# A sample's recurrence in two wide units, shift states stored in rows, and a layer norm in the dense PSUM banks

## The chip, the cores and the metric

The kernel runs on one core of a Trainium2 chip. The metric is the time on the device of one execution, in microseconds (us), less being better. A core has five engines with an instruction queue each: TensorE (PE in the profile, with its weight loads as PEld), VectorE (DVE), ScalarE (ACT), GpSimd (POOL) and SyncE (SP), which here issues nearly all the DMAs. Each engine takes its instructions in order, and waits between engines go by semaphores. Matmul results land in PSUM, eight banks of 128 partitions by 512 fp32 numbers, from where DVE and ACT read them.

## The reference

One step of a two-layer encoder, on a new prompt of 1024 tokens and on 64 further tokens of a running stream, the sample, whose states are inputs. The model is 1024 wide. Layer 0 mixes tokens by two recurrences side by side, RWKV-7 with eight heads of 64 and a gated linear attention (GLA) with four heads, both fed by one input projection; their outputs, joined, go through one output projection. Layer 1 mixes them by attention over a band of chunks. Behind each mixer stand a residual with a layer norm, a SwiGLU feed-forward part (FFN), and again a residual with a layer norm. Besides the two outputs, all end states are returned. The change touches the recurrence, two of its returned states and one layer norm.

```python
def wkv7_scan(r, decay, k, v, kk, a, S0):
    def step(S, inp):
        r_t, w_t, k_t, v_t, kk_t, a_t = inp
        sa = jnp.einsum('bhvk,bhk->bhv', S, kk_t)
        S = (S * w_t[:, :, None, :] - sa[..., None] * (kk_t * a_t)[:, :, None, :]
             + v_t[..., None] * k_t[:, :, None, :])
        return S, jnp.einsum('bhvk,bhk->bhv', S, r_t)
...
def rwkv7_time_mix(pa, shift0, wkv0, mu, ...):
    prev = jnp.concatenate([shift0[:, None, :].astype(pa.dtype), pa[:, :-1]], axis=1)
    xs = pa + (prev - pa) * mu
    ...
    wkv, o = wkv7_scan(r, decay, k, v, kk, a, wkv0)
    ...
    return y, wkv.astype(wkv0.dtype), pa[:, -1]
```

`pa` is the part of the input projection that feeds RWKV, 1792 columns. Its last row, `pa[:, -1]`, is the **shift state**, returned once for the prompt and once for the sample.

## The kernel before

*Halves.* The tokens are worked in two halves. Half 0 holds the first 384 prompt tokens and the 64 of the sample (448 columns), half 1 the other 640 prompt tokens. `run` (L1340) writes the program down in this order: input projection of half 0, the scan of half 0 beside the rest of its projection, input projection of half 1, output projection of half 0 with layer norm ln1, FFN of half 0 with the scan of half 1 beside it, and so on. The Tile scheduler then sets the order of the instructions on each engine by its own model of time, so that instructions of parts that are independent mix.

*Dense matmuls.* Each is split into fp32r high and low parts and done as three products: `gemm_ws` (L124 to L126, weights stationary) and `gemm_ts` (L135 to L138, tokens stationary), with weights loaded by SP (L98) and split by ACT (L101), DVE (L106) and POOL (L108). They write in a pool of three PSUM banks, which `self.bank()` hands out (tile name gps). The output projection adds into the accumulators acc (L825, L827 and L829), which are loaded from the input by SP (acc<-in_x).

*The recurrence.* `rwkv` (L656) splits the eight heads into four pairs p and the tokens into chunks of 64. A unit is one pair and n chunks. Units go through a pipeline of five steps, one step of each of five units in a round: `rw1` (L412: loads rkv, xg and rsb through SP, gate matmuls in the bank pa, elementwise work), `rw1b` (products in pb and pt), rw2 (an inverse of triangular 16 by 16 blocks: the write of lab to l_d in DRAM, its diagonal blocks read back as lt, and 15 rounds of a DVE product and sum, L549 and L551; more in pz), `rw3` (L599: the state S goes through the unit's chunks in the bank ps) and `rw4` (L645: output y, written to yg_d). For the prompt n is 2, one pair and two chunks, so all tiles are 128 wide. The sample has one chunk: four units of n = 1, one for each pair, 64 wide, which stand ahead of the prompt's units of half 0. With three pairs of chunks in half 0 and five in half 1, there are 4 + 12 + 20 = 36 units. A step of the GLA (`gla`, tiles named g...) is drawn beside each round.

*Scan banks.* The scan has PSUM banks of its own, by tags: pa, pb and pt share one, pz has one, ps and py share two, and everything else, the GLA's and "tps", shares one. `self.tpsum` says where the transposes of a layer norm (L902) and a few others land: from L1350 on in the bank "tps". ACT (L113) and DVE (L114) then split them into xh and xl for the next matmuls.

*Shift states.* `shift_evac` copies the last column of each of the 14 projection tiles into a column of a tile of 128 by 14: shS in half 0 (the sample's), shP in half 1 (L290). At the end of half 1's projection both are stored as 1792 numbers, transposed by the DMA's access pattern (L1377 and L1378). The scheduler moves the store of shS ahead to 92 us.

*What follows half 1's projection.* SP has the write rkv_d<-xs (L303), the loads of the scan (rkv, L427; xg; rsb), loads and stores of the value cache (cv, L1125, and vd, L1128, with ACT's and DVE's split of cv as cvh), the read of yg_d as yraw, whose split xh (L215) and xl (L216) is the output projection's input, and the loads of acc.

## Time and profile before

| what | before |
|---|---|
| runs (us) | 3109.51, 3102.37, 3113.97; median 3109.51 |
| the profiled execution: time, span (us) | 3102.95, 3101.2 |
| mean granted TensorE clock | 0.977 |
| DMA packets, bytes | 298492, 399.29 MB (mean 129 GB/s) |
| share of the chain that ended last, by engine | PE 77%, DVE 8%, DMA 7%, POOL 2%, ACT 2%, issue 2%, SP's queue 1% |

The span runs from the first to the last instruction. A busy time is the sum over an engine's instructions; PE and PEld overlap. The granted clock is the share of full speed that the throttle allowed PE. A group's line gives the line of the code, the engine, the operation and its tiles. "<-" in a list of waits names what ended an engine's idle time. The chain of waits is followed back from the last instruction: at each step to what released it, or to the instruction before it on its engine.

### The profile page before, as it was taken

The page shows a single profiled execution, that of the slowest core. Times are in us where ns is not written, and L with a number is a line of the kernel's source. Part 1 is how long each engine was busy: PE and PEld are TensorE (multiplying, and loading weights), DVE is VectorE, ACT ScalarE, POOL GpSimd, SP SyncE. Part 2 cuts the span into 40 slices and gives each one's busy share as a digit, 9 for nine tenths or more (in the row PEclk, how much of TensorE's full clock was granted, in tenths as well). Part 3 has the DMA queues.
Part 4 walks back from the last instruction along what each step waited for, and adds up shares of the span by engine and source line. Part 5 has one row for each costly group of instructions (what it writes and reads, how often), then busy time and mean ns, then how long its engine had stood idle before and what let it go on. Part 6 is the DMA issues. An engine that isn't in the chain of part 4 may idle for free.

```text
span 3101.2 us, 50069 instructions
## 1 busy us (share of the span) xinstructions
PE 3007.5 (97%) x17468; PEld 2676.5 (86%) x17468; DVE 2016.0 (65%) x4941; ACT 1270.8 (41%) x2761; POOL 1366.7 (44%) x1489
## 2 busy tenths in 40 slices
PE   8999999899999999999999999999999999899998
PEld 7888888688888888798999898898899988899987
DVE  5677875879898764455554466245566668866667
ACT  4454554344454334243443132355444434333322
POOL 2354534444454334343342233244445546654444
PEclk9999999889999999999999999999899999999999
DMA  6553334533533228343342222866454443322212
GB/s 195 148 161 115 109 110 124 146 104 106 151 105 106 91 97 294 118 153 120 113 134 98 82 95 101 247 200 175 121 153 135 117 175 122 122 86 80 98 68 75
DMA packets 298492, 399.29 MB, mean 129 GB/s; under 512 B 125504, under 2 KB 218552, under 8 KB 298240
## 3 DMA queue, kind: packets, MB, share of 16 engines
q1 hardware_dynamic: 297088, 393.48, 41.2%
q8 instruction: 138, 2.26, 0.3%
q10 hardware_dynamic: 1152, 2.62, 0.2%
q14 instruction: 114, 0.93, 0.1%
HBM read 323.63 MB, written 75.51 MB: 129 GB/s over the span
## 4 chain that ended last, share of the span: by engine, by line
PE 77%; DVE 8%; DMA 7%; POOL 2%; issue 2%; ACT 2%; SPq 1%; POOLq 0%; ACTq 0%; DVEq 0%
PE gps L124 11%; PE gps L126 11%; PE gps L125 11%; PE gps L135 7%; PE gps L136 7%; PE gps L138 7%; PE gps L1065 3%; PE gps L1066 3%; PE gps L1067 3%; PE op L1328 2%; PE tp L1302 2%; DVE t L549 1%; DVE x L551 1%; PE sps L1286 1%; PE sps L1287 1%
## 5 line engine op out<-in xcount | busy, mean ns | idle before, releaser
L108 POOL TENSOR_TENSOR wl<-wr,wh 128x512 fp32r<-128x512 f32 (+2 forms) x297 | 521.7, 1760 | 669.3 <-ACT wh L101 612.0
L124 PE MATMUL gps<-xh,wh 128*128 128x320 f32 (+1 forms) x2188 | 747.7, 342 | 12.5 <-ACT xh L215 6.0
L125 PE MATMUL gps<-xl,wh 128*128 128x320 f32 (+1 forms) x2188 | 746.5, 341 | 0.6 <-DVE xl L216 0.6
L126 PE MATMUL gps<-xh,wl 128*128 128x320 f32 (+1 forms) x2188 | 745.9, 341 | 0.3 <-DVE wl L106 0.2
L101 ACT CAST wh<-wr 128x1024 fp32r<-128x1024 f32 x360 | 375.6, 1048 | 465.9 <-PE gps L125 135.6
L106 DVE TENSOR_TENSOR wl<-wr,wh 128x512 fp32r<-128x512 f32 (+2 forms) x297 | 293.8, 990 | 242.2 <-ACT wh L101 239.8
L124 PEld LDWEIGHTS gps<-xh,wh 128*128 128x128 f32 x2188 | 415.6, 190 | 34.4 <-ACT xh L215 6.0
L126 PEld LDWEIGHTS gps<-xh,wl 128*128 128x128 f32 x2188 | 415.6, 190 | 18.6 <-issue 0.8
L125 PEld LDWEIGHTS gps<-xl,wh 128*128 128x128 f32 x2188 | 415.5, 190 | 18.3 <-DVE xl L216 1.0
L1297 POOL TENSOR_SCALAR s<-s,mx 128x640 f32<-128x640 f32 (+5 forms) x144 | 205.3, 1426 | 258.7 <-DVE mx L1296 236.3
L138 PE MATMUL gps<-wh,xl 128*128 128x512 f32 x661 | 258.9, 397 | 5.4 <-DVE xl L216 4.8
L135 PE MATMUL gps<-wh,xh 128*128 128x512 f32 x661 | 259.9, 399 | 3.9 <-DVE acc L829 1.9
L136 PE MATMUL gps<-wl,xh 128*128 128x512 f32 x661 | 261.5, 397 | 0.0
L135 PE MATMUL gps<-wh,hh 128*128 128x512 f32 x572 | 224.8, 396 | 1.6 <-ACT wh L101 1.3
L136 PE MATMUL gps<-wl,hh 128*128 128x512 f32 x572 | 225.5, 396 | 0.0
L827 DVE TENSOR_TENSOR acc<-acc,gps 128x512 f32<-128x512 f32 x216 | 143.6, 680 | 89.6 <-PE gps L138 82.3
L138 PE MATMUL gps<-wh,hl 128*128 128x512 f32 x484 | 189.6, 397 | 1.6 <-DVE hl L943 1.6
L549 DVE TENSOR_TENSOR t<-lt,x 16x48 f32<-16x48 f32 (+9 forms) x540 | 149.3, 276 | 36.0 <-DMA lt<-l_d 25.5
L1295 ACT ACTIVATE s<-s,mx 128x640 f32<-128x640 f32 (+5 forms) x144 | 96.4, 669 | 149.6 <-DVE mx L1294 145.2
L138 PEld LDWEIGHTS gps<-wh,xl 128*128 128x128 f32 x661 | 124.9, 189 | 33.8 <-DVE xl L216 5.4
L135 PEld LDWEIGHTS gps<-wh,xh 128*128 128x128 f32 x661 | 125.0, 190 | 32.8 <-issue 2.5
L136 PEld LDWEIGHTS gps<-wl,xh 128*128 128x128 f32 x661 | 125.2, 189 | 28.0 <-DVE wl L106 1.1
(406 smaller groups left out, 6312.0 us busy)
## 6 DMA issues: line engine op xcount, KB each, us to landing
wr<-in_w_fi SPq DMA_DIRECT2D x176, 512.0 KB
wr<-in_w_fo SPq DMA_DIRECT2D x88, 512.0 KB
wr<-in_w_in SPq DMA_DIRECT2D x44, 512.0 KB
wr<-in_w_qk SPq DMA_DIRECT2D x32, 512.0 KB
wr<-in_w_o SPq DMA_DIRECT2D x24, 512.0 KB
qs<-qd SPq DMA_DIRECT2D x32, 320.0 KB
wr<-in_w_om SPq DMA_DIRECT2D x16, 512.0 KB
wr<-in_w_v SPq DMA_DIRECT2D x16, 512.0 KB
```

Of the source, the lines that this page charges most:

```text
L101: self.A.copy(hi, raw)
L106: self.V.tensor_tensor(lo[:, :h], raw[:, :h], hi[:, :h].bitcast(F32), op=ALU.subtract)
L108: self.G.tensor_tensor(lo[:, h:], raw[:, h:], hi[:, h:].bitcast(F32), op=ALU.subtract)
L124: self.T.matmul(ps, hi[:, kt, :], xh, start=(kt == 0), stop=False)
L125: self.T.matmul(ps, hi[:, kt, :], xl, start=False, stop=False)
L126: self.T.matmul(ps, lo[:, kt, :], xh, start=False, stop=(kt == nk - 1))
L135: self.T.matmul(ps, xh, wh, start=(i == 0), stop=False)
L136: self.T.matmul(ps, xh, wl, start=False, stop=(lo is None and i == n - 1))
L138: self.T.matmul(ps, cols(lo(kt)), wh, start=False, stop=(i == n - 1))
L549: V.tensor_tensor(tv, lt[:, j, w:16].unsqueeze(2).to_broadcast([m, r, w]), x[:, 0, j, 0:w].unsqueeze(1).to_broadcast([m, r, w]), op=ALU.mult)
L827: self.V.tensor_tensor(a, a, ps[:m], op=ALU.add)
L1297: G.tensor_scalar(s[:m, :nk], s[:m, :nk], mx[:m, 3:4], None, op0=ALU.mult)
```

## The change

It has three parts. The line numbers of the kernel after are up to 22 higher; a line that is only moved is named by its new number.

1. The sample's recurrence runs in two units of two pairs each (p = 0 and 1, then 2 and 3) instead of four of one. Such a unit is 128 wide, like the prompt's. In `rw1`, `rw3`, `rw4` and `rwkv` a unit has segments, one for each pair, with loads, activations with a bias by pair, and states by segment. In `rw3` each segment starts from its own state.
2. shS and shP become columns 0 to 13 and 14 to 27 of one tile, shO. At the end of half 1's projection PE transposes it (L1394) into a dense bank, ACT copies it, and two DMAs store 14 rows of 128 numbers each (L1397, L1398).
3. During the output projection of half 0 `self.tpsum` is `self.bank`, so that ln1's transposes (L918 now) land in the three dense banks. Behind it `tpsum` is set back.

```diff
         self.shA = pool.tile([128, 14], F32, name="shA", tag="shA")
-        self.shS = pool.tile([128, 14], F32, name="shS", tag="shS")
-        self.shP = pool.tile([128, 14], F32, name="shP", tag="shP")
+        self.shO = pool.tile([128, 28], F32, name="shO", tag="shO")
+        self.shS, self.shP = self.shO[:, 0:14], self.shO[:, 14:28]
...
-    def rw1(self, sp, p, n, g0):
+    def rw1(self, sp, ps, n, g0):
-        W = 64 * n
-        u = SimpleNamespace(p=p, n=n)
-        pc = slice(128 * p, 128 * p + 128)
+        w = 64 * n
+        W = w * len(ps)
+        n *= len(ps)
+        u = SimpleNamespace(n=n, segs=[(p, slice(w * i, w * i + w)) for i, p in enumerate(ps)])
...
-        gs = slice(g0, g0 + W)
+        gs = slice(g0, g0 + w)
         rkv = sp.tile([128, 3, W], F32, tag="rkv", name="rkv", bufs=3)
-        nc.sync.dma_start(rkv, self.rkv_d[:, p, :, gs].rearrange("a p t -> p a t"))
+        for p, cs in u.segs:
+            nc.sync.dma_start(rkv[:, :, cs], self.rkv_d[:, p, :, gs].rearrange("a p t -> p a t"))
         r, k, v = rkv[:, 0, :], rkv[:, 1, :], rkv[:, 2, :]
-        xg = sp.tile([128, 2, W], F32, tag="xg", name="xg", bufs=2)
+        xg = sp.tile([128, 2, w], F32, tag="xg", name="xg", bufs=2)
         nc.sync.dma_start(xg, self.xg_d[:, :, gs].rearrange("a p t -> p a t"))
         rsb = st("rsb", bufs=2)
-        for h in range(2):
-            src = self.rs_d[2 * p + h : 2 * p + h + 1, gs]
-            nc.sync.dma_start(rsb[QH[h]], bass.AP(tensor=src.tensor, offset=src.offset, ap=[[0, 64], [1, W]]))
+        for p, cs in u.segs:
+            for h in range(2):
+                src = self.rs_d[2 * p + h : 2 * p + h + 1, gs]
+                nc.sync.dma_start(rsb[QH[h], cs], bass.AP(tensor=src.tensor, offset=src.offset, ap=[[0, 64], [1, w]]))
         pa = self.sbank("pa")
-        T.matmul(pa[:, 0:W], self.w2z[:, pc], xg[:, 0, :], start=True, stop=True)
-        T.matmul(pa[:, W : 2 * W], self.a2z[:, pc], xg[:, 0, :], start=True, stop=True)
-        T.matmul(pa[:, 2 * W : 3 * W], self.g2[:, pc], xg[:, 1, :], start=True, stop=True)
...
+        for p, cs in u.segs:
+            pc = slice(128 * p, 128 * p + 128)
+            for i, (m, x) in enumerate(((self.w2z, 0), (self.a2z, 0), (self.g2, 1))):
+                T.matmul(pa[:, W * i + cs.start : W * i + cs.stop], m[:, pc], xg[:, x, :], start=True, stop=True)
+        for p, cs in u.segs:
+            A.activation(th[:, cs], pa[:, cs], AF.Tanh, bias=self.w0h[:, p : p + 1], scale=0.5)
+            A.activation(tha[:, cs], pa[:, W + cs.start : W + cs.stop], AF.Tanh, bias=self.a0h[:, p : p + 1], scale=0.5)
...
     def rw3(self, sp, u, S):
-        G.tensor_copy(u.sv[0:64, 0], S)
+        step = n // len(u.segs)
+        for i, (p, _) in enumerate(u.segs):
+            G.tensor_copy(u.sv[0:64, i * step], S[p])
+        out = {}
...
-            S2 = u.sv[0:64, c + 1] if c + 1 < n else sp.tile([64, 2, 64], F32, tag=f"S{p}", name="S", bufs=2)
+            p = u.segs[c // step][0]
+            if (c + 1) % step:
+                S2 = u.sv[0:64, c + 1]
+            else:
+                S2 = out[p] = sp.tile([64, 2, 64], F32, tag=f"S{p}", name="S", bufs=2)
...
     def rwkv(self, hf, sp, n, src, S):
 
-        units = [(p, n, 64 * c, 0) for c in range(0, (PA, NB)[hf] // 64, n) for p in range(4)]
+        units = [((p,), n, 64 * c, 0) for c in range(0, (PA, NB)[hf] // 64, n) for p in range(4)]
         if hf == 0:
-            units = [(p, 1, SMP, 1) for p in range(4)] + units
+            units = [((p, p + 1), 1, SMP, 1) for p in (0, 2)] + units
             S += [self.state(sp, p, self.a["wkv0"]) for p in range(4)]
         else:
             S += [self.state(sp, p, src) for p in range(4)]
         st = {}
         def one(i):
-            p, m, c0, smp = units[i]
-            st[i] = self.rw1(sp, p, m, self.base[hf] + c0)
+            ps, m, c0, smp = units[i]
+            st[i] = self.rw1(sp, ps, m, self.base[hf] + c0)
 
         def three(i):
-            p, m, c0, smp = units[i]
-            S[p] = self.rw3(sp, st[i], S[p])
-            if smp:
-                self.wkv_out(sp, S[p], self.a["s_wkv"][2 * p : 2 * p + 2])
-                S[p] = self.state(sp, p, src)
-            elif hf == 0 and c0 == PA - 64 * n:
-                self.nc.sync.dma_start(self.wkv_d[p].rearrange("(h k) v -> k h v", h=2), S[p])
+            ps, m, c0, smp = units[i]
+            for p, s in self.rw3(sp, st[i], S).items():
+                S[p] = s
+                if smp:
+                    self.wkv_out(sp, s, self.a["s_wkv"][2 * p : 2 * p + 2])
+                    S[p] = self.state(sp, p, src)
+                elif hf == 0 and c0 == PA - 64 * n:
+                    self.nc.sync.dma_start(self.wkv_d[p].rearrange("(h k) v -> k h v", h=2), s)
...
         self.inproj_gla(1, one)
         self.inproj_rwkv(1, one)
-        nc.sync.dma_start(a["s_shift"].rearrange("c p -> p c"), self.shS)
-        nc.sync.dma_start(a["p_shift"].rearrange("c p -> p c"), self.shP)
+        ps = self.bank()[:28, :128]
+        self.T.transpose(ps, self.shO, self.ident)
+        t = one.tile([128, NM], F32, tag="sq", name="sho", bufs=3)[:28, :128]
+        self.A.copy(t, ps)
+        nc.sync.dma_start(a["s_shift"], t[0:14])
+        nc.sync.dma_start(a["p_shift"], t[14:28])
         es_one.close()
         self.load_xt(0, self.yg_d, (4, 5, 6, 7, 0, 1, 2, 3), pool=yp)
@@ -1396,7 +1416,9 @@
             next(r)
             next(g)
+        self.tpsum = self.bank
         self.proj(0, acc0, "w_om", self.layer_norm(0, acc0, "ln1", 0), pa)
+        self.tpsum = lambda: self.sbank("tps")
         for _ in r:
             next(g, None)
         for _ in g:
```

The order of the instructions changes with it, since the scheduler places all again. First SP, between the last write of half 1's rows (rkv_d<-xs) and the loads behind it. Here vd and cv are the value cache, wr the weights of the output projection, rkv and yg_d the scan's, gb the layer norm's weights. Before:

```order
L1128 DMA vd<-cvh 128x512
L1125 DMA cv<-in_ck_v 128x4x64
L303 DMA rkv_d<-xs 128x640
L1378 DMA out_dram<-shP 128x14x1
L98 DMA wr<-in_w_om 128x1024
L427 DMA rkv<-rkv_d 128x3x128
L654 DMA yg_d<-y 128x128
L1128 DMA vd<-cvh 128x512
L1125 DMA cv<-in_ck_v 128x4x64
```

and now:

```order
L303 DMA rkv_d<-xs 128x640
L98 DMA wr<-in_w_om 128x1024
L889 DMA gb<-in_ln_w 128x1024
L1397 DMA out_dram<-sho 14x128
L1398 DMA out_dram<-sho 14x128
L429 DMA rkv<-rkv_d 128x3x128
L889 DMA gb<-in_ln_b 128x1024
L429 DMA rkv<-rkv_d 128x3x128
L1144 DMA vd<-cvh 128x512
L1141 DMA cv<-in_ck_v 128x4x64
L813 DMA acc<-in_x 128x1024 x3
L813 DMA acc<-in_x 64x1024
```

The store of shP stood right behind the write rkv_d<-xs and ahead of the loads of rkv and cv. Now two stores of rows stand there, behind the loads of wr and gb; the load of acc has come nearer. The store of shS is no longer at its early place.

The second place is PE inside the output projection, around the second and third block of ln1's transposes (L902; a tile of 128 tokens has two blocks of four). ps, pz and pt are the scan's tiles. Before:

```order
L902 MATMUL tps<-ident,acc 128x128 x4
L618 MATMUL ps<-uv,tok 64x64 x2
L621 MATMUL ps<-sv,ro 64x64
L622 MATMUL ps<-uv,arb 64x64
L621 MATMUL ps<-sv,ro 64x64
L622 MATMUL ps<-uv,arb 64x64
L577 MATMUL pz<-tt,lab 128x64 x2
L902 MATMUL tps<-ident,acc 128x128 x4
L584 MATMUL pz<-btt,yb 128x64 x2
L509 MATMUL pt<-ident,bk 128x128 x2
L510 MATMUL pt<-th,bdk 128x128
L511 MATMUL pt<-ident,rkv 128x128
```

and now:

```order
L756 MATMUL gps<-gv,gkt 128x128
L583 MATMUL pz<-tt,lab 128x64 x2
L590 MATMUL pz<-btt,yb 128x64 x2
L918 MATMUL gps<-ident,acc 128x128 x4
L515 MATMUL pt<-ident,bk 128x128 x2
L516 MATMUL pt<-th,bdk 128x128
L517 MATMUL pt<-ident,rkv 128x128
L918 MATMUL gps<-ident,acc 128x128 x4
L135 MATMUL gps<-wh,xh_69 128x512
L136 MATMUL gps<-wl,xh_69 128x512
L138 MATMUL gps<-wh,xl_70 128x512
```

Before, matmuls of rw2 and rw3 stand between the blocks, and the blocks write in tps. Now they write in gps, two blocks stand nearer to each other, and the projection matmuls of the next token tile (L135 to L138) follow them in the same three banks.

The third place is DVE in the same stage, from one tile's layer norm (L892, L897; now L908, L913) to the next accumulation. L549 and L551 (now L555 and L557) are rw2's rounds. Before:

```order
L892 SCALAR_TENSOR_TENSOR acc<-acc,mv,gb 128x512 x2
L549 TENSOR_TENSOR t_7243<-lt,x_7242 16x15
L587 COPY_PREDICATED btt<-u_191,pz 128x2x64
L758 SCALAR_TENSOR_TENSOR gy<-gpy,gnwh,gsg 128x128
L897 SCALAR_TENSOR_TENSOR acc<-acc,rstd,gb 128x512
L827 TENSOR_TENSOR acc<-acc,gps 128x512
L551 TENSOR_TENSOR x_7242<-x_7242,t_7243 16x15
L520 TENSOR_TENSOR bon<-pt,rkv 128x128
L884 BN_STATS bs<-acc 128x6
L552 COPY x_7242<-x_7242 16x256
L827 TENSOR_TENSOR acc<-acc,gps 128x512
```

and now, ahead of the next accumulation (L843):

```order
L555 TENSOR_TENSOR t_7833<-lt,x_7832 16x28
L114 TENSOR_TENSOR xl_70<-gps,xh_69 128x4x128
L557 TENSOR_TENSOR x_7832<-x_7832,t_7833 16x14x2
L465 TENSOR_TENSOR ar<-kkn,eb 128x2x64
L555 TENSOR_TENSOR t_7833<-lt,x_7832 16x39
L114 TENSOR_TENSOR xl_70<-gps,xh_69 128x4x128
L467 SCALAR_TENSOR_TENSOR kkn<-tha,kkn 128x128
L557 TENSOR_TENSOR x_7832<-x_7832,t_7833 16x13x3
L468 SCALAR_TENSOR_TENSOR bk<-kkn,enb 128x2x64
L555 TENSOR_TENSOR t_7833<-lt,x_7832 16x48
L451 SCALAR_TENSOR_TENSOR kkn<-rkv,vec,rsb 128x128
L843 TENSOR_TENSOR acc<-acc,gps 128x512
```

More of the scan's rows stand between: from the last copy into the shift tile (L290) to the last xl of ln1, DVE has 226 rows before and 324 now, and PE's rows of the second half's scan begin eight units ahead of the first FFN matmul, where six were. From about a third of the program on, the two orders are nearly alike.

29 lines of the change are left out of this document (15 added, 14 removed).

## The prediction

> **What bounds the kernel now.** I read the page first (share of the span and instructions of each engine).
>
> ```profile
> PE 3007.5 (97%) x17468; PEld 2676.5 (86%) x17468; DVE 2016.0 (65%) x4941; ACT 1270.8 (41%) x2761; POOL 1366.7 (44%) x1489
> ```
>
> TensorE (PE) is busy nearly all the time. So time is won only where PE stands still, runs at a low clock, or does work that could stand in such a place. Next I read the view of busy time by stretches around the places that the diff touches. Its columns are the length of the stretch; PE, weight loads, DVE, ACT and POOL (busy us, instructions); then PE clock, DMA share, GB/s.
>
> ```profile
> 106.00:112.00 6.00, 5.15 (x29) 4.42 (x27) 2.42 (x10) 2.04 (x5) 4.03 (x4) 1.00 0.65 205
> 112.00:118.00 6.00, 5.36 (x22) 4.77 (x23) 5.45 (x25) 4.28 (x12) 1.42 (x3) 0.72 0.65 207
> 539.80:641.90 102.10, 86.28 (x426) 70.13 (x425) 84.01 (x232) 37.22 (x105) 51.07 (x70) 0.77 0.52 140
> 545.00:550.00 5.00, 3.67 (x20) 2.87 (x18) 1.36 (x7) 0.00 (x0) 0.00 (x0) 1.00 0.99 50
> 550.00:555.00 5.00, 0.00 (x0) 0.00 (x0) 0.00 (x0) 0.00 (x0) 0.00 (x0) 0.66 0.69 179
> 555.00:565.00 10.00, 6.53 (x28) 5.78 (x29) 7.68 (x26) 5.11 (x17) 4.06 (x10) 0.50 0.77 235
> 565.00:605.00 40.00, 40.00 (x210) 32.93 (x208) 37.53 (x94) 13.69 (x38) 20.39 (x25) 1.00 0.53 152
> 605.00:615.00 10.00, 5.53 (x32) 4.85 (x32) 9.94 (x19) 5.15 (x12) 6.87 (x5) 0.73 0.34 119
> 615.00:640.00 25.00, 23.46 (x114) 18.08 (x113) 20.90 (x60) 11.94 (x36) 16.40 (x24) 0.50 0.32 111
> 700.00:1000.00 300.00, 297.49 (x1890) 254.06 (x1890) 267.54 (x885) 143.04 (x439) 151.33 (x253) 0.99 0.40 116
> ```
>
> From 700 to 1000 us (first FFN, with the second part's scan beside it) PE is the bound: 297.49 of 300. I call 539.8 to 641.9 us the **seam**: from shP's last copy to the end of the first layer norm, with the output projection between. There DVE sets the pace from 565 on, 37.53 of 40 and then 9.94 of 10 us, and from 550 to 555 no engine works at all. The chain of waits that ended last in this window (its five longest pieces in order of time: start, length, what) and its row for the first accumulation say why.
>
> ```profile
> 539.88 9.74 DMA rkv_d<-xs
> 550.13 4.35 DMA yg_d<-y
> 554.50 2.44 DMA yraw<-yg_d
> 557.56 0.63 DVE xl L216
> 558.22 5.18 DMA acc<-in_x
> ```
>
> ```profile
> 565.25 0.60 DVE acc L825
> ```
>
> The timeline has shP's last copy and its store (durations, first and last start), and the list of waits the one that follows (total, times, longest).
>
> ```profile
> L290 DVE COPY shP<-gps x1: 134/134/134, 539.8 to 539.8; 128x1 f32<-128x1 f32 x1
> L1378 SPq DMA_DIRECT2D out_dram<-shP x1: 424/424/424, 540.4 to 540.4; - x1
> ```
>
> ```profile
> ACT cvh L113 <- DMA cv<-in_ck_v: 11.9, 1, 11.9
> ```
>
> The store goes out half a microsecond behind the write rkv_d<-xs and turns shP: 128 x 14 = 1,792 single elements. The write beside it takes 9.74 us. SP waits for that write at its next load of rkv, so the load of cv, queued behind, is late and ACT waits 11.9 us for it.
>
> **The change, part by part.** *Stores in rows.* The DMA view of 541.0 to 549.6 us:
>
> ```profile
> DMA packets 2234, 0.67 MB, mean 78 GB/s; under 512 B 2040, under 2 KB 2040, under 8 KB 2233
> q1 hardware_dynamic: 2233, 0.65, 93.1%
> ```
>
> 2,040 small packets hold the DMA engines at 93.1% for 8.6 us. The new stores are 28 rows of 512 B, so this goes. DVE's idle time from 545 to 565 us is 3.64 + 5.00 + 2.32 = 11.0 us. What is late next is DVE's own work: from shP's last copy to the first accumulation it took 565.25 - 539.78 = 25.5 us, and without 11.0 us 14.5. I take **-11**. The upper end is -6: the five pieces of the chain stay in their order, rkv_d<-xs shrinks to some 4 us, and the loads of yraw and acc come no earlier. The lower is -13, if the 2.4 us of DVE in front overlap too.
>
> The Trainium skill, "DMA: Bandwidth & Descriptors", section "Why small descriptors are slow (HBM only)", speaks against this term: it gives a fixed overhead of about three cycles a packet, from which I estimate some 0.5 us for 1,792 packets over 16 engines, and the term would be near nothing. The trace has 8.6 us of full engines, and the row decides.
>
> The new store adds one PE transpose ahead of the output projection, which waits for the copy of the last column, and an ACT copy. Projection matmuls that stood ahead of that copy now stand behind it: PE may be held some 2 us, but it waits for the accumulators later anyway. That costs 0 while the accumulators are later than the transpose, +2 otherwise. On SP the two row stores wait for ACT's copy, with the loads of rkv, cv and acc queued behind: 0 to +1, inside the -6 above.
>
> *The same store of shS* stands at 92 us. The chain there:
>
> ```profile
> 92.70 13.36 DMA wr<-in_w_gv
> 106.12 1.53 DMA l_d<-lab
> ```
>
> A 512 KB weight load took 13.36 us, and the scan's write l_d came right behind it. PE stands still for 0.85 + 0.64 us from 106 to 118 us, and loses 6 x 0.28 = 1.7 us by the clock: **-3**, with 0 if the scan's own chain of steps sets that gap, and -5 if the loads ahead of 106 us gain too.
>
> *The sample in two units.* The scan has two units fewer. The price of a unit comes from the view by stretches up to 1100 us, for the PSUM tiles ps, pz, pb, pa and pt in this order (PE, weight loads, DVE, and ACT last where given; pa has no DVE), and from the groups of DVE instructions (columns: count, then busy us and mean ns, then idle before).
>
> ```profile
> 0.00:1100.00 1100.00, 155.51 (x1348) 109.08 (x1348) 30.92 (x134) 42.82 (x171) 0.96 0.43 126
> 0.00:1100.00 1100.00, 97.71 (x680) 93.41 (x680) 55.65 (x180) 9.22 (x36) 0.96 0.43 126
> 0.00:1100.00 1100.00, 42.29 (x272) 38.60 (x272) 63.66 (x180) 0.96 0.43 126
> 0.00:1100.00 1100.00, 34.02 (x216) 29.71 (x216) 0.00 (x0) 29.11 (x108) 0.96 0.43 126
> 0.00:1100.00 1100.00, 26.90 (x176) 21.09 (x176) 9.73 (x36) 30.41 (x104) 0.96 0.43 126
> ```
>
> ```profile
> L549 DVE TENSOR_TENSOR t<-lt,x 16x48 f32<-16x48 f32 (+9 forms) x540 | 149.3, 276 | 36.0 <-DMA lt<-l_d 25.5
> L551 DVE TENSOR_TENSOR x<-x,t 16x48 f32<-16x48 f32 (+9 forms) x540 | 141.3, 262 | 10.9
> ```
>
> ```profile
> L725 PE MATMUL gpa<-gqk,gbqk 128*128 128x64 f32 x68 | 13.4, 280 | 0.0
> ```
>
> The five PE columns sum to 356.4 us over 36 units (each has 15 instructions of L549, 540 / 36): 9.9 us each. A step of the gated linear attention, issued beside each unit, has four matmul groups like L725's, 34 steps in all: about 4 x 13.4 / 34 = 1.6 us. On DVE L549 and L551 are 290.6 / 36 = 8.1 us a unit whatever its width, and the tiles' columns 160.0 / 36 = 4.4 us.
>
> The sample's PE work itself does not shrink, since a wide unit does the matmuls of two, and the DVE time freed before 500 us lies under a busy PE and is worth nothing. What counts is that the scan runs ahead. In the order of the program eight units of the second part have begun ahead of the first FFN matmul, where six had. So behind the seam, where PE is the bound (297.49 of 300), two units and two steps fewer stand: 2 x (9.9 + 1.6) = 23.0 us. Their tails cross the border in both orders; I take **-21**, between -17 and -25.
>
> The price is paid in the seam, where DVE sets the pace. From shP's last copy to the last xl of the layer norm DVE has 226 rows in the order of before and 324 in that of the change. The 98 more are nearly all the scan's, at 0.25 us (the rows' own means by line, L549 and L551 above 0.26 to 0.28 and short copies below) to 0.36 us (84.01 / 232): 24.5 to 35. I take **+24**, by the scan's own lines, which these rows are, and leave DVE's idle share as it is; +12 if the gaps of 2.47 + 4.10 us from 565 to 640 and part of those ahead of 565 are filled. Nothing covers the rest: each row stands ahead of an instruction that the layer norm needs.
>
> *The layer norm in the dense banks.* Its transposes now have one bank, shared with the gated attention. The view of that tile (durations, first and last start; at its foot the idle time that its reader or writer ended):
>
> ```profile
> L902 PE MATMUL tps<-ident,acc x32: 272/392/477, 599.4 to 640.4; 128*128 128x128 f32 x24, 64*128 64x64 f32 x8
> L113 ACT CAST xh<-tps x8: 357/574/587, 602.2 to 640.7; 128x512 fp32r<-128x512 f32 x6, 128x256 fp32r<-128x256 f32 x2
> L114 DVE TENSOR_TENSOR xl<-tps,xh x8: 394/672/692, 604.7 to 641.2; 128x512 fp32r<-128x512 f32 x6, 128x256 fp32r<-128x256 f32 x2
> ...
>   PE tps L902: 3.3, 4
>   DVE xl L114: 1.1, 2
> ```
>
> The waits around it are 3.3 + 1.1 = 4.4 us, so at most -4. Against it: three banks serve both the projection and these transposes. Scan matmuls that stood between the transposes no longer do, and the next 24 projection matmuls (half a token tile) may stand behind the reads of the tile before. The timeline has them at the full clock:
>
> ```profile
> L135 PE MATMUL gps<-wh,xh x36: 387/389/497, 567.2 to 598.8; 128*128 128x512 f32 x36
> ```
>
> 24 x 0.389 = 9.3 us; if half of it is not covered, 4.7 us at each of three tile borders, 14 in all. From -4 to +14, I take **0**, near the row of waits, since PE and DVE have scan rows to do meanwhile.
>
> **Sum**: -11 - 3 + 24 - 21 + 0 = **-11**. The profiled execution took 3102.95 us (a span of 3101.2 and 1.75 around it): 3092. It lies 6.6 us under the median of 3109.51, so for a median I add that: 3098.5, **3098**. A measurement of this kernel tells about 0.5%, 15.5 us, from no change, so this lies inside.
>
> **Rivals.** *More gain* (33%): the seam closes up. Clock 0.50 from 615 to 640 us cost PE 12.5 us, and DVE idled 4.1 there. If the scan's rows keep PE and DVE at work, the +24 shrinks to +8 (24 less 2.47 + 4.10 us of idle and 9 of the 12.5): -27, **3082**. For it: no stretch without work remains. Against: the added DVE rows are on the engine that already sets the pace.
>
> The Trainium skill, "TensorE: Matmul & The Clock Gate", section "What's actually happening", has the clock rise after one busy window of about 3.4 us. The trace has PE busy 23.46 of 25 us at 0.50 all the while, so a rule that short would favour this rival more than the row does.
>
> *No gain* (15%): the third part doesn't do what it says. The wait for one bank becomes PE's wait for the layer norm ahead of each tile's matmuls, with a fifth of the 14 filled: +11, and the sum is 0, **3109**. For it: the scan stands no more between the transposes. Against: its rows are only moved ahead.
>
> *Slower* (8%): the same coupling at half clock. PE, idle at each tile border, stays at 0.50, the matmuls take twice as long, and the price is 28 instead of 14: 3098 + 28 = **3126**. It decides from a slip of 26.5 us, 9 a border, where the time passes 3125. For it: 0.50 stood in this place before (615 to 640). Against: PE has to be idle between, with 98 more rows of scan on hand.
>
> [...]
>
> **How the numbers follow.** Forecast 44%, with its own range 3090 to 3106, a quarter of it beyond the bound; more gain 33%, nine tenths of it beyond; no gain 15%; slower 8%. Faster by over 0.5% (under 3094): 0.11 + 0.30 = 0.41; slower: 0.08 and 0.01 of the one before: 0.09; within: 0.50. The lower end takes the favourable ends together, -13 - 5 + 12 - 25 - 4 = -35, less 2 because they won't all fall so, and 6 for the spread of the runs (3102.37 to 3113.97): 3070. The upper takes the unfavourable ones of two terms beside the forecast of the rest, +35 in place of +24, half of the coupling's 14 and SP's +1: 8 above the median, 3118. Only the slower rival and the tails lie outside.
>
> **What would show it.** In the new profile: no stretch with all engines idle near 550 us, and rkv_d<-xs well under 9.74 us; the first accumulation within 16 us of the last copy into shO (-11 right); the layer norm's last xl some 13 us later against that copy than the 101.4 of now, with DVE busy above 90% between (+24); the scan's last unit some 20 us earlier (-21). A layer norm that ends no later than now is the first rival, one 24 us later the second. The forecast is wrong if PE isn't the bound behind the seam, or if the rest, whose order is nearly the same, runs otherwise.

## The result, and the profile after

The changed kernel is slower: 3126.09 us median of 5 runs (3121.81 to 3126.66), before 3105.07 us (5 runs, 3102.37 to 3113.97). The ratio is 1.0061, with a 95% interval from 1.0048 to 1.0074. That lies outside the predicted range of 3070 to 3118, on the other side of the forecast. The profiled execution took 3121.81 us, its span 3120.0, so 18.8 us more than the span of before.

The page's first line of after shows that PE is the bound as before:

```profile
PE 3014.8 (97%) x17461; PEld 2681.7 (86%) x17461; DVE 1995.0 (64%) x4837; ACT 1268.4 (41%) x2732; POOL 1355.8 (43%) x1463
```

DVE has 104 instructions fewer, as the two missing units would have it, and PE nearly the same number as before. Where the 18.8 us arise is read from three rows of the timeline (durations, then first and last start): the last copy into the shift tile, the last xl of ln1, and further on the last transposes of ln2, which stand behind the first FFN and the second half's scan. After:

```profile
L290 DVE COPY shO<-gps x8: 134/142/148, 483.0 to 548.9; 128x1 f32<-128x1 f32 x8
L114 DVE TENSOR_TENSOR xl<-gps,xh x8: 405/676/691, 612.4 to 676.1; 128x512 fp32r<-128x512 f32 x6, 128x256 fp32r<-128x256 f32 x2
L918 PE MATMUL ps<-ident,acc x12: 223/272/273, 1170.4 to 1191.8; 128*128 128x128 f32 x8, 64*128 64x64 f32 x4
```

Before, the last row is

```profile
L902 PE MATMUL ps<-ident,acc x12: 222/272/273, 1155.3 to 1175.4; 128*128 128x128 f32 x8, 64*128 64x64 f32 x4
```

and the last starts of the other two are 539.8 and 641.2. This gives four stages (us, from last start to last start), which every experiment below is read by:

| stage | before | after | difference | forecast |
|---|---|---|---|---|
| ahead of the seam, to the last shift copy | 539.8 | 548.9 | +9.1 | -3 |
| the seam, to the last xl of ln1 | 101.4 | 127.2 | +25.8 | -11 + 24 + 0 |
| behind it, to ln2's last transposes | 534.2 | 515.7 | -18.5 | -21 |
| the rest | 1925.8 | 1928.2 | +2.4 | 0 |

Each stage is read from one execution, and single executions spread. Four kernels below have the row stores and the four narrow units, and their first 3212 PE matmuls stand in the order of before: their last copy comes between 0.1 us earlier and 5.9 us later than that of before. So differences of some 6 us ahead of the seam say little.

In the seam the first accumulation of after starts 13.7 us behind the last copy (562.6 - 548.9):

```profile
L841 DVE SCALAR_TENSOR_TENSOR acc<-acc,gps x8: 668/672/689, 562.6 to 587.2; 128x512 f32<-128x512 f32 x6, 64x512 f32<-64x512 f32 x2
```

What no longer stands there is the slow write: four writes rkv_d<-xs from 520 to 560 us take 2.1 to 4.2 us each from issue to landing, where one took 9.74 before. The chain of waits has the new store of rows in that stretch instead, 5.37 us, and behind it the load of acc, which is issued as that store lands (at 556.5) and takes 6.00.

From the first accumulation to the end of ln1 the view by stretches has, first for before, then for after (columns as in the prediction):

```profile
563.50:599.40 35.90, 35.74 (x181) 29.58 (x182) 33.43 (x88) 11.23 (x33) 18.55 (x24) 0.98 0.59 175
599.40:641.90 42.50, 36.49 (x183) 29.02 (x182) 38.18 (x97) 19.91 (x52) 26.43 (x33) 0.62 0.31 104
```

```profile
562.60:610.60 48.00, 40.94 (x227) 32.55 (x228) 38.61 (x110) 18.52 (x58) 23.11 (x35) 0.86 0.47 127
610.60:676.50 65.90, 56.93 (x298) 47.33 (x297) 58.20 (x175) 29.13 (x90) 36.78 (x60) 0.73 0.28 77
```

DVE is busy 96.81 us instead of 71.61, 25.2 more. But it also idles 17.1 us instead of 6.8, and PE 16.0 instead of 6.2: neither is the bound alone now, they take turns. The chain that ended last shows it (start, length, engine, tile and line; L918 are ln1's transposes, L135 and L138 the projection, L843 its accumulation, L905 and L908 steps of the layer norm):

```profile
610.84 1.71 PE gps L918 x8
612.55 0.43 PE gps L135
...
619.15 0.24 PE gps L138
619.41 0.69 DVE acc L843
...
622.48 1.32 DVE acc L908 x2
...
627.89 0.85 PE gps L918 x4
628.75 0.43 PE gps L135
...
639.12 2.54 POOL rstd L905
...
644.62 0.83 PE gps L918 x4
```

Transposes of a tile, the next tile's 24 projection matmuls, their accumulation, that tile's statistics, its transposes, the next 24 matmuls: one chain through PE, DVE and POOL, with the scan's instructions in its gaps. Before, the same matmuls ran in one pass, and the layer norm followed at its own pace. The row of L138 in the timeline shows that, before and after (the window of after also holds one matmul of the first pass more):

```profile
L138 PE MATMUL gps<-wh,xl x36: 387/389/502, 567.8 to 599.8; 128*128 128x512 f32 x36
```

```profile
L138 PE MATMUL gps<-wh,xl x37: 388/393/628, 560.0 to 635.6; 128*128 128x512 f32 x37
```

The kernel's code gives a reason, which is argued and not shown. The three banks are handed out in turn. In the second pass of the projection (the one that ln1 follows) each tile takes four: two for the halves of its columns, and two for its blocks of transposes. So the second half of the next tile gets the bank of this tile's first block and has to wait until that block is read, and in PE's queue the next tile's matmuls stand behind both blocks. The scheduler put the scan into these gaps. I read the 98 more DVE rows as the trace of the wait and not as its cause: by the traces the seam has 226 rows before, 229 with wide units and row stores, 324 with all three parts, and 201 with all three but other banks. No run keeps the rows and takes the wait away.

### The profile page after: what moved, and what is told of

Read it like the earlier page. It is cut to its first block, busy times and chain, and to the rows that moved or that the text cites. A ratio compares the mean times of both kernels' runs of the same rounds, so it can differ in the third digit from the quotient of the medians.

```text
span 3120.0 us, 49880 instructions
## 1 busy us (share of the span) xinstructions
PE 3014.8 (97%) x17461; PEld 2681.7 (86%) x17461; DVE 1995.0 (64%) x4837; ACT 1268.4 (41%) x2732; POOL 1355.8 (43%) x1463
## 4 chain that ended last, share of the span: by engine, by line
PE 74%; DVE 10%; DMA 8%; POOL 2%; issue 2%; ACT 2%; SPq 1%; POOLq 0%; DVEq 0%; ACTq 0%
PE gps L124 10%; PE gps L126 10%; PE gps L125 10%; PE gps L135 8%; PE gps L136 8%; PE gps L138 7%; PE gps L1081 2%; PE gps L1083 2%; PE gps L1082 2%; PE op L1344 2%; PE tp L1318 2%; DVE x L557 1%; DVE t L555 1%; DMA wr<-in_w_in 1%; PE sps L1302 1%
## 5 line engine op out<-in xcount | busy, mean ns | idle before, releaser
L125 PEld LDWEIGHTS gps<-xl,wh 128*128 128x128 f32 x2188 | 414.9, 190 | 18.8 <-DVE xl L216 1.0
L135 PE MATMUL gps<-wh,xh 128*128 128x512 f32 x661 | 260.9, 401 | 4.2 <-DVE acc L845 1.8
L138 PE MATMUL gps<-wh,xl 128*128 128x512 f32 x661 | 260.4, 398 | 0.5 <-DVE xl L114 0.5
L135 PE MATMUL gps<-wh,hh 128*128 128x512 f32 x572 | 224.9, 397 | 1.1 <-DVE acc L843 0.6
L843 DVE TENSOR_TENSOR acc<-acc,gps 128x512 f32<-128x512 f32 x216 | 143.6, 680 | 100.5 <-PE gps L138 91.1
L138 PE MATMUL gps<-wh,hl 128*128 128x512 f32 x484 | 187.6, 394 | 0.0
L555 DVE TENSOR_TENSOR t<-lt,x 16x15 f32<-16x15 f32 (+7 forms) x510 | 135.4, 265 | 38.1 <-DMA lt<-l_d 28.3
L135 PEld LDWEIGHTS gps<-wh,xh 128*128 128x128 f32 x661 | 126.0, 191 | 32.5 <-issue 2.3
L138 PEld LDWEIGHTS gps<-wh,xl 128*128 128x128 f32 x661 | 125.5, 190 | 29.0 <-DVE xl L114 1.0
```

Source lines behind the costliest of these rows:

```text
L125: self.T.matmul(ps, hi[:, kt, :], xl, start=False, stop=False)
L135: self.T.matmul(ps, xh, wh, start=(i == 0), stop=False)
L138: self.T.matmul(ps, cols(lo(kt)), wh, start=False, stop=(i == n - 1))
L555: V.tensor_tensor(tv, lt[:, j, w:16].unsqueeze(2).to_broadcast([m, r, w]), x[:, 0, j, 0:w].unsqueeze(1).to_broadcast([m, r, w]), op=ALU.mult)
L843: self.V.tensor_tensor(a, a, ps[:m], op=ALU.add)
```

## The experiments

In the tables, "ratio" is that of a kernel's runs to those of before on the same chip, and the four stages are those above, as differences to before (us, one profiled execution). Medians of before beside these runs were 3103.99 to 3106.14 us.

**The parts, one by one.** First the row stores alone (`shO`, the transpose and two row DMAs, with the rest of before):

> Only the second part: the shift states go through PE and are stored in rows; the sample keeps its four units and the layer norm its one bank. The banks theory says that the 19 us come from the third part, because the layer norm's transposes in the dense banks let the scheduler put some 90 DVE rows of the scan ahead of them. The units theory says that they come from the first part, because PE waits inside the longer chain of a wide unit. Both say the same of this run: 11 to 14 us less than before, with no stretch without work near 550 us; the order has 225 DVE rows from the last shift copy to the last xl of the layer norm, 227 before, so nothing is paid back.

Then one line about the output projection:

```diff
+        self.tpsum = self.bank
         self.proj(0, acc0, "w_om", self.layer_norm(0, acc0, "ln1", 0), pa)
+        self.tpsum = lambda: self.sbank("tps")
```

> Only the third part: the first layer norm's transposes in the dense banks. The order has 281 DVE rows from the last shift copy to the last xl where before has 227, and six units of the second half begun ahead of the first FFN matmul, as before. Banks theory: 54 rows at 0.25 us are 13 us in the seam, little of it repaid, and the idle of the stall near 550 us stays: 10 to 18 us more than before. Units theory: within 4 us of before.

The wide units alone (`rw1`, `rw1b`, `rw3`, `rw4` and `rwkv` of after), and the same with the row stores:

> Only the first part: the sample in two wide units, with the elementwise stores and the layer norm's one bank. The order has 233 DVE rows in the seam and seven units begun ahead of the first FFN matmul, where before has six. Banks theory: one unit and GLA step fewer behind the seam for no more rows in it, 11 us less than before, or down to no change if the wide units lose on the way to the seam. Units theory: 20 to 30 us more than before, since the stall near 550 us stays too.

> The first and second part, with the layer norm in its one bank, so the change without its third part. The order has 230 DVE rows in the seam, against 325 with the third part. Banks theory: 20 to 25 us less than before, some 40 less than the changed kernel. Units theory: within 5 us of the changed kernel, so 15 to 20 more than before.

And the second and third part without the first:

> The second and third part without the wide units, as the change has them (the transpose's bank is counted). If the parts add, -5 and +17 give 10 to 14 us more than before. If the third part costs less once the stall near 550 us is gone, 3 to 8 more. Units theory: what is left of the changed kernel's 20 us is the wide units' own, so this is at least 8 us under the changed kernel.

| parts | median | ratio, interval | ahead | seam | behind | rest |
|---|---|---|---|---|---|---|
| rows | 3100.97 | 0.9983 (0.9972 to 0.9994) | +3.5 | -6.0 | -1.2 | +4.7 |
| dense banks | 3122.84 | 1.0061 (1.0038 to 1.0085) | +2.9 | +20.0 | +0.1 | -3.4 |
| wide units | 3124.49 | 1.0061 (1.0042 to 1.0080) | +18.7 | +2.5 | -7.1 | +2.2 |
| wide, rows | 3120.12 | 1.0042 (1.0028 to 1.0056) | +10.3 | +0.6 | -4.9 | +12.2 |
| rows, dense | 3115.57 | 1.0027 (1.0017 to 1.0037) | -0.1 | +20.6 | -12.8 | +4.1 |
| all three | 3126.09 | 1.0061 (1.0048 to 1.0074) | +9.1 | +25.8 | -18.5 | +2.4 |

Only the row stores gain, and less than both theories said. The dense banks cost 20.0 to 26.6 us in the seam: 20.0 alone, 26.6 on top of the row stores (122.0 against 95.4), 25.2 on top of both other parts (127.2 against 102.0). Alone nothing of it comes back behind the seam; on top of the others 11.6 and 13.6 us do, as more of the scan has run by then. In the medians they cost 16.7 us alone, 14.6 on top of the row stores, and 6.0 on top of both.

But the wide units cost too, which the banks theory denied: 18.4 us alone, 19.2 on top of the row stores, 10.5 on top of both other parts. With them the last copy comes 6.8 us later (wide, rows against rows), 9.2 (all three against rows, dense) or 18.7 (alone). So each theory was half right: either of the two, put on top of the row stores, makes the kernel slower than before. Rows and dense banks nearly add (-5.2 and +16.7 give 11.5, measured 9.9); with the wide units they don't, -5.2 + 16.7 + 18.4 would be 30 where 21 was measured.

One candidate for why the row stores gain only 5 us is in the waits of PE between 535 and 700 us (total, times, longest); a run below tries it:

```profile
PE ps L611 <- ACT sv L517: 3.5, 1, 3.5
PE gps L1378 <- DVE shO L290: 3.4, 1, 3.4
```

The stall near 550 us is gone: the first accumulation starts at 559.0, 15.7 us behind the last copy, where it took 23.7. In its place PE stands for 6.9 us ahead of the projection: the transpose (L1378 here) is in PE's queue ahead of the projection matmuls, and it waits for the last copy.

**The banks.** The changed kernel with other banks for ln1's transposes, those of the scan's tag c:

```diff
-        self.tpsum = self.bank
+        self.tpsum = lambda: self.sbank("py")
```

> The changed kernel with the layer norm's transposes in the two banks of the recurrence's ps and py instead of the three dense ones; all else as changed. Coupling theory: in the dense banks the next token tile's 24 projection matmuls wait for the layer norm of the tile before, and the scan's rows only fill the gaps. With other banks the second half of the projection runs in one pass again, the seam from the last shift copy to the last xl falls from 128 us to 95 to 108, and the run is 8 to 14 us more than before. Rival: the scan's lead of the wide units makes the seam long whatever the banks: seam above 118 us, within 5 us of the changed kernel.

3109.61 us, ratio 1.0015 (1.0005 to 1.0024), 16.5 us less than the changed kernel. The seam is 84.6 us long, shorter than the coupling theory had it:

```profile
L114 DVE TENSOR_TENSOR xl<-py,xh x8: 407/672/694, 609.3 to 636.4; 128x512 fp32r<-128x512 f32 x6, 128x256 fp32r<-128x256 f32 x2
```

```profile
565.40:637.00 71.60, 56.24 (x301) 45.93 (x301) 65.98 (x162) 27.34 (x70) 41.59 (x50) 0.88 0.41 118
```

DVE is busy 65.98 of 71.60 us again, with the wide units in place. Together with the 102.0 us of wide, rows in the old bank, that settles the seam: the dense banks cost it, not the scan's lead. But the stage behind takes 542.7 us, 8.5 more than before and 27.0 more than in the changed kernel. So most of the 42.6 us that the seam is shorter is paid back there, and the seam's length alone doesn't price the run.

At half dose, on the kernel of before, one block of transposes in the dense banks and one in its old bank:

> The third part alone, at half dose: of the two blocks of transposes of a token tile one goes to the dense banks and one stays in its old bank (the count of banks is kept as the third part leaves it, modulo 8). With one block the three banks leave the projection two, so that it may run one tile ahead of the layer norm. Coupling theory: the seam from the last shift copy to the last xl lies between before (102 us) and the whole third part (122 us), 107 to 117, and the run 5 to 12 us above before, against 17. Rival: any use of the dense banks costs all of it, as the order has 274 DVE rows there (281 with the whole part): seam above 118, 14 to 18 us above before.

3118.71 us, ratio 1.0036 (1.0024 to 1.0048), with a seam of 117.7. Seam and time (13 us over before) lie between the two theories, so the run decides for neither. One block a tile already gives 16.3 of the 20.0 us. By the code a tile takes three of the three banks here, so no half of a projection gets a bank that a block has used. Yet PE's timeline has the next tile's projection right behind the dense block (start, length):

```profile
603.64 1.06 PE L902 MATMUL gps<-ident,acc 128*128 128x128 f32 x4
604.35 0.78 PE L135 MATMUL gps<-wh,xh 128*128 128x512 f32 x1
```

So a bank that is still to be read can't be the whole reason. That the scheduler keeps to the turn in which the banks are handed out would explain both runs; no run tests it alone. The last two have no wide units and other banks (with the edits of the next part):

> No wide units: the row stores with the count kept, and the layer norm's transposes in the two banks of ps and py. In the changed kernel these banks shortened the seam from 128 to 85 us. Coupling theory: seam 85 to 95 here too, where the row stores alone have 96, but the scan's work that the seam no longer holds comes behind it, so 0 to 6 us less than with the row stores and the kept count, 8 to 14 less than before. Rival: ps needs its two banks, and the scan behind the seam is late by more than the seam wins: 0 to 6 us less than before.

> As the run before, with the transpose of the shift states behind the projection. If the two edits add, 10 to 16 us less than before; if they fill the same idle time of PE, 8 to 11 less, as each of them.

3097.81 us (0.9967, 0.9955 to 0.9979) and 3100.19 (0.9983, 0.9974 to 0.9993). The seam is 92.1 us in both, but the stage behind it 541.1 and 538.9, where before had 534.2. Other banks shorten the seam and lengthen what follows: neither kernel is faster than the same one with the old bank (3096.51 and 3094.00, below), and the two edits don't add.

**The count of banks, and the place of the transpose.** `bank()` counts its calls, and in the last stage, where a second pool (gp2) is open, the count modulo 8 says which pool a tile comes from. The third part adds eight calls, the stores one.

```diff
         ps = self.bank()[:28, :128]
+        self.bcount -= 1
```

> As the run with the row stores alone, but the bank that the new transpose takes is not counted. The count (bcount, modulo 8) decides in the last stage which of two pools each dense tile takes its PSUM bank from, and the stores shift it by one. Counter theory: the last 4509 rows of PE's order are those of before again, the 4.4 us that the row stores lose behind 2400 us are gone, and the run is 8 to 10 us faster than before, against 5 with the count shifted. Chance theory: what is lost there has nothing to do with the count, 3 to 6 us faster than before, as without this edit.

> The changed kernel with the same edit, the transpose's bank not counted. Counter theory: 4 to 5 us less than the changed kernel, 14 to 17 more than before, with no difference to before in the stages behind 2400 us. Chance theory: within 2 us of the changed kernel, 19 to 21 more than before.

Row stores: 3096.51 us, ratio 0.9969 (0.9958 to 0.9980), the rest at 1924.1 where it was 1930.5. Changed kernel: 3118.60, ratio 1.0039 (1.0025 to 1.0052), the rest at 1925.8 where it was 1928.2. In both traces the last 4742 PE matmuls stand in the order of before again, and the medians fall by 4.5 and 7.5 us, as the counter theory has it. But each pair's intervals overlap, and single executions spread as much: the nine kernels that keep the count of before, itself included, have 1921.5 to 1931.4 us for the rest (mean 1926.0), the eight with the count shifted 1927.2 to 1938.0 (mean 1930.5). So the count is worth some 4.5 us, as an estimate from these means, and that both kernels land so near to before is partly luck.

Then the transpose behind the output projection, its copy in a tile of the scan:

```diff
         self.proj(0, acc0, "w_om", self.layer_norm(0, acc0, "ln1", 0), pa)
+        ps = self.bank()[:28, :128]
+        self.bcount -= 1
+        self.T.transpose(ps, self.shO, self.ident)
+        t = sc.tile([128, 128], F32, tag="y", name="y", bufs=1)[:28]
```

> The row stores with the count kept, and the transpose written behind the output projection instead of ahead of it, its copy in a buffer of the scan. In the run with the row stores PE stood still for 7.0 us ahead of the projection, waiting for the scan's rows and then for the last copy into the shift tile. Queue theory: the transpose in PE's queue holds the projection matmuls behind it; without it 5 to 8 us more come off, 14 to 17 less than before. Rival: PE has nothing else that is ready there and the idle only moves, so as without this edit, 8 to 10 less than before.

3094.00 us, ratio 0.9963 (0.9952 to 0.9975): the fastest of all, 10.7 us under before, and faster than both kernels. Over the edit before it is 2.5 us, not 5 to 8, and the intervals overlap: the rival has it. The two waits ahead of the projection went, but one of 4.8 us for an xl (L216) stands in their place, as it does before, and the seam grew by 1.6 us (97.6 against 96.0). So nothing here shows that the transpose's place keeps the row stores from more.

**What the wide units cost.** All three with row stores and without the dense banks; first the rounds of the scan that are written ahead of the GLA's projection:

```diff
-        for _ in range(4):
+        for _ in range(3):
             next(r)
```

> The wide units with row stores (without the dense banks), but three instead of four rounds of the scan written ahead of the gated attention's projection. Four rounds now hold two wide units and two prompt units, where they held four narrow ones. Early-load theory: the wide units cost because the same rounds put more of the scan's work beside the first projection, where PE has to wait for its chain; with three rounds the last shift copy comes back from 550 us to 543 to 547, and the run is 6 to 12 us faster than with four. Rival: the price is that of the wide chain itself, wherever it stands: last copy at 549 to 553, within 4 us of four rounds, 11 to 19 more than before.

> As the run before, with two rounds. The order has 268 DVE rows in the seam and six units begun ahead of the first FFN matmul, as with narrow units. Early-load theory: the last copy at 538 to 545 us, but what was ahead now stands in the seam, which is 5 to 15 us longer: 0 to 8 us less than with four rounds. Rival: last copy at 548 to 553 and the seam longer all the same, 5 us or more slower than with four rounds.

```diff
-            units = [((p, p + 1), 1, SMP, 1) for p in (0, 2)] + units
+            units = [((0, 1), 1, SMP, 1), ((2,), 1, SMP, 1), ((3,), 1, SMP, 1)] + units
```

> With row stores and without the dense banks: the first two pairs of the sample in one wide unit, the other two in narrow ones, so three units. The order already has seven units begun ahead of the first FFN matmul, as with two wide units, and 230 DVE rows in the seam. If the price of wide units grows by the unit, half of it: 7 to 11 us slower than with row stores alone, last copy at 546 to 548 us. If it comes with the unit that runs ahead into the seam, as much as with two wide units: 15 to 20 slower. If the price is a matter of how the scheduler's order falls out, no rule: anything from 0 to 20.

| kernel | median | ratio, interval | last copy | seam |
|---|---|---|---|---|
| rows, no wide units | 3100.97 | 0.9983 (0.9972 to 0.9994) | 543.3 | 95.4 |
| two wide, four rounds | 3120.12 | 1.0042 (1.0028 to 1.0056) | 550.1 | 102.0 |
| two wide, three rounds | 3112.34 | 1.0033 (1.0020 to 1.0046) | 553.7 | 94.1 |
| two wide, two rounds | 3110.69 | 1.0024 (1.0015 to 1.0034) | 531.7 | 107.2 |
| one wide, two narrow | 3122.42 | 1.0062 (1.0047 to 1.0077) | 561.0 | 102.2 |

One wide unit costs as much as two, so there is no price by the unit. Three rounds won 8 us, but not where the early-load theory said: the last copy came at 553.7. Two rounds moved it to 531.7, earlier than expected, and gave part of that back in the seam. The price depends on where the rounds fall, up to about half of it. A part of that is seen from 400 to 500 us: all five kernels with two wide units and four rounds have PE busy 94.01 to 94.03 us there, where before has 97.93, row stores 97.94, and two wide units with two rounds 98.08. The longest waits of PE there are for the scan (wide, rows; total, times, longest):

```profile
PE ps L620 <- DVE sv L638: 2.1, 1, 2.1
PE pb L490 <- DVE x L557: 1.7, 1, 1.7
```

The other half, some 10 us over the row stores alone, stays open, and no run has fewer rounds with narrow units, so what the rounds alone are worth isn't known. Every kernel with wide units is slower than before, and none shows the gain that I gave them.

## Why the prediction was wrong

- **The dense banks, 0: the first step that failed.** I took the waits around the old bank (4.4 us) as the measure and "near the row of waits" as the value, "since PE and DVE have scan rows to do meanwhile". They had, and did them, and the layer norm waited: 20.0 to 26.6 us in the seam, and in the medians 16.7 us alone, 14.6 on top of the row stores, 6.0 on top of both other parts. The mechanism, PE's wait for the layer norm ahead of each tile's matmuls, is what I named under *no gain* at +11, and again at half clock under *slower*. That the time came out at the 3126 of *slower* is luck: its clock of 0.50 didn't come (0.86 and 0.73 in the two stretches), and its sum had neither the right price for this part nor that of the wide units. I gave it 8%, though the order quoted ahead of the prediction shows the coupling: a block of transposes, and the next tile's projection matmuls directly behind it, in the same three banks.
- **The rows of DVE, +24.** The size was right (25.2 us more busy time), the cause wrong. I put them down to the wide units; the order of those alone has 233 rows in the seam and that of the dense banks alone 281, where before has 227. I counted the order of the whole change and not of its parts. And I left "DVE's idle share as it is": its idle time rose by 10.3 us, which the sum doesn't have.
- **Two units fewer behind the seam, -21: the second step that failed.** Measured -18.5, so the number is near, by luck: the wide units give 5.7 of it (all three against rows, dense), and rows, dense has -12.8 with no unit fewer. With the +24 I priced the wide units at +3 and put nothing ahead of the seam; the runs have them at 10.5 to 19.2 us, with the last copy 6.8 to 18.7 us later. PE's work is the same in both kernels (17468 and 17461 matmuls), so a unit that runs earlier is won only where PE stood still. Ahead of the seam all three have 33 matmuls more than before at the last copy:

```profile
0.00:539.80 539.80, 513.38 (x3220) 447.17 (x3221) 380.59 (x1287) 269.44 (x708) 222.28 (x369) 0.97 0.47 137
```

```profile
0.00:548.90 548.90, 519.16 (x3253) 450.56 (x3253) 371.25 (x1233) 272.19 (x702) 224.98 (x358) 0.97 0.46 136
```

  That is 5.8 us more PE work and 3.3 more idle in the 9.1 us; my sum held PE's share ahead of the seam at nothing. What else the wide units cost stays open by about half, as said above.
- **The stall of shP, -11.** Right: -10.0 (and -8.0 with the row stores alone). (The row of before that I quoted at 565.25 was the second accumulation. The first started at 563.5, as the timeline has it,

```profile
L825 DVE SCALAR_TENSOR_TENSOR acc<-acc,gps x8: 667/674/689, 563.5 to 580.0; 128x512 f32<-128x512 f32 x6, 64x512 f32<-64x512 f32 x2
```

  so the stretch was 23.7 us, and 13.7 after.) The signs that I named for it came too: no stretch without work, and the write rkv_d<-xs well under 9.74 us. The transpose, which I costed at 0 to +2, held PE for 1.0 us in the changed kernel and for 3.4 us in the run with the row stores alone. The Trainium skill, "DMA: Bandwidth & Descriptors", "Why small descriptors are slow (HBM only)", gave some 0.5 us for these packets by my estimate; the runs go with the row of 8.6 us, not with it.
- **The store of shS, -3.** Not seen: with the row stores and narrow units the last copy comes 0.1 us earlier to 5.9 later in four kernels. The last section has the rows.
- **The rest, 0.** The count of banks was not in the sum. The trace of after has 2.4 us more there, which is within the spread of single executions.

Together: +9.1 - 10.0 + 35.8 - 18.5 + 2.4 = +18.8, where 35.8 is from the first accumulation to the last xl (113.5 against 77.7).

The Trainium skill, "TensorE: Matmul & The Clock Gate", "A second HAM failure mode: psum-queue depth-cycling", tells of a clock that swings when PE idles between groups that go round through the banks. The clock in the two stretches fits only in part: it cost 0.14 x 48.0 + 0.27 x 65.9 = 24.5 us here, but 0.02 x 35.9 + 0.38 x 42.5 = 16.9 before, without that cycling.

## What to carry to other kernels

When two stages share a pool of buffers that goes round, write down which buffer each takes in turn, and read in the engine's order whether the first stage's next piece stands behind the second stage's last one: then the stages are chained. Work that a scheduler moves ahead costs the same engine the same time there; count a gain only for idle time that it fills, and count the order of each part of a change by itself. And look for counters: one more call of an allocator can turn the choice of buffers in a stage that nobody touched.

## What the runs showed of the hardware

The stall that I meant to win back at the store of shS moved instead of going, and its clock loss with it. The view by stretches has for before:

```profile
88.00:92.00 4.00, 4.00 (x25) 2.55 (x24) 2.13 (x6) 2.09 (x5) 2.63 (x2) 1.00 0.59 201
92.00:106.00 14.00, 13.84 (x70) 11.85 (x68) 7.98 (x24) 12.11 (x27) 6.20 (x15) 1.00 0.75 77
106.00:118.00 12.00, 10.51 (x51) 9.19 (x50) 7.86 (x34) 6.32 (x17) 5.45 (x7) 0.86 0.65 206
```

and for the row stores alone:

```profile
88.00:92.00 4.00, 1.09 (x8) 0.77 (x7) 2.94 (x9) 2.11 (x10) 2.90 (x4) 0.93 0.38 132
92.00:106.00 14.00, 14.00 (x52) 11.05 (x53) 7.31 (x22) 10.76 (x22) 5.61 (x13) 0.78 0.32 98
106.00:118.00 12.00, 12.00 (x65) 10.61 (x64) 10.26 (x32) 7.03 (x17) 4.85 (x8) 1.00 0.50 165
177.00:201.00 24.00, 23.93 (x95) 17.65 (x96) 19.06 (x62) 14.31 (x37) 15.02 (x31) 0.51 0.46 138
```

From 106 to 118 PE now works all the time at full clock, as forecast. But from 88 to 92 it is idle for 2.91 us, where before has no idle time, and behind that the clock from 92 to 106 is 0.78. The three other kernels with the row stores, narrow units and the transpose ahead of the projection have the same: PE idle for 1.95 to 2.55 us from 88 to 94, and a clock of 0.76. The two with the transpose behind the projection have 1.00 from 92 on, and full clock from 106 to 118 too. Why the transpose's place would matter so early was not tried, and chance has a share: the half-dose kernel, with the old stores and PE's first 3392 matmuls in the order of before, has 0.88 from 92 to 106 and full clock from 106 to 118.

The last row is a fact of its own: for 24 us the clock was 0.51 with PE busy 23.93 us, so in this trace a busy PE alone did not bring the clock back soon. That stretch is not the row stores' doing: from 160 to 200 us the six kernels with row stores and narrow units have a mean clock of 0.71 to 0.87, and three with the old store 0.79 to 0.87.
